# Layer 0's dense MLP on one core: half-width seven-product blocks for three quarters of its first product

## The chip, the cores and the metric

The kernel runs on one core of one Trainium2 chip. Its five engines work in parallel and meet through semaphores: TensorE (PE in the profile; its weight loads are listed apart as PEld), VectorE (DVE), ScalarE (ACT), GpSimd (POOL) and SyncE (SP), which here only issues DMAs. The metric is the device time of one execution in microseconds; the reference point is the median of the timed runs of the kernel before.

## The reference

512 tokens of width 1024 pass two pre-norm residual layers, each a token mixer followed by a dense MLP with a squared ReLU. The part that changes is layer 0's MLP:

```python
def squared_relu_mlp(h, w1, w2):
    a = jax.nn.relu(h @ w1)          # h: 512 x 1024, w1: 1024 x 4096
    return (a * a) @ w2              # w2: 4096 x 1024

    h = rmsnorm(x, norm_ffn_g[i])
    x = x + squared_relu_mlp(h, mlp_w1[i], mlp_w2[i])
```

All data is float32.

## The kernel before

**Three matmuls for one.** A float32 product is made of rounded fp32r parts. Each operand is split into a high part and a remainder, and `mm3` issues three matmuls: high x high, high x low, low x high. Of a weight piece of 128 x 1024 values, ScalarE makes the high part (`nc.scalar.copy(out=p.hi, ...)`, tile wH), and VectorE the remainder (`nc.vector.tensor_sub(out=p.lo, ...)`, tile wL). The matmuls hold a 128x128 block of the weight piece in the array and stream 512 tokens past it: 128x512 is one matmul's output, in one PSUM bank.

**Steps and look-ahead.** The program is a list of `steps`; nearly every step consumes one weight piece (24 matmuls). `run` of a step issues its matmuls, then `advance()` (second halves of earlier evacuations), then `refill()`, and last its own evacuation. `refill` prepares wH up to three and wL up to two pieces ahead:

```python
    def refill():
        n = pos["done"]
        prep(n + (LOOK if n >= 4 else 1), n + (LOOK - 1 if n >= 4 else 1))
```

The order of the calls is the order in each engine's queue, and each engine works its queue in that order. `prep` also loads raw weights, 1 MB each (`load_raws`, `load_part`, on SP's queue), into the pool `bigp` of 14 rotating buffers of 8 KB per partition. The normalised input of a layer lies in `hH` and `hL` (high and remainder, 8 tiles each, in the pool `keep`).

**Layer 0's MLP.** `up(0, q)` makes a quarter (1024 features) of `relu(h @ w1)` in eight steps of 128 features x 512 tokens, each a sum of 8 products over the 1024 inputs; `evac_a` squares it and splits it into `aH` and `aL`. `down(0, q)` multiplies that quarter with w2: eight steps of 128 outputs, each a sum over the quarter's 1024 inputs, so that a step ends in one accumulator. `evac_x(scaled=True)` adds each to the residual `xT`, times the squared norm factor `r2bc` (the factor of the norm is left out of `h` and put back here): two VectorE instructions, `xs` and `xT`. The accumulators are PSUM banks of two pools: `acc` (6) and `mis` (2). In the last `down` each evacuation also makes the next layer's `hH`, `hL` and squares. The order is up 0, up 1, down 0, up 2, down 1, up 3, down 2, down 3. After it the program goes on with `v_unit(0)` of the retention mixer.

Layer 1's MLP already has a Strassen form (`seven`): its VectorE instructions on 128x512 halves (`sa`, `sd`: sums of blocks; `sp`: remainder of such a sum after ScalarE's cast) are of the kinds that the change brings to layer 0.

Of the kernel before, what the change touches and what calls it, by code (L numbers as in the profile page):

```python
# [32 lines left out]
class Raw:  # L33
# [3 lines left out]
    def __init__(self, src, parts=1, adds=(), over=None):  # L37
        self.src, self.parts, self.tile, self.done = src, parts, None, 0
        self.adds, self.over, self.split = adds, over, 0


class Piece:


    def __init__(self, raw, view, shape):
        self.raw, self.view, self.shape = raw, view, shape
        self.hi = self.lo = None
# [33 lines left out]
def trunk(ctx, tc, x, norm_mix_g, norm_ffn_g, a_w_in, a_b_in, a_v_norm_g, a_w_s, a_b_s, a_w_out,  # L81
# [6 lines left out]
    bigp = ctx.enter_context(tc.tile_pool(name="bigp", bufs=14))  # L88
# [4 lines left out]
    ahead = {"raws": 2}  # L93
# [42 lines left out]
    hH = [keep.tile([P, T], F32R, name=f"hH{k}") for k in range(KD)]  # L136
    hL = [keep.tile([P, T], F32R, name=f"hL{k}") for k in range(KD)]
# [18 lines left out]
    def load_part(r):  # L156
        if r.tile is None:
            r.tile = big([P] + list(r.src.shape[1:]), F32, f"raw{raws.index(r)}")
# [5 lines left out]
    def load_raws(upto):  # L164
        while pos["raw"] < min(upto, len(raws)):
            r = raws[pos["raw"]]
            if r.over is not None:
                if r.over.split < 2:
                    return
                r.tile, r.done = r.over.tile, r.parts  # L170
            while r.done < r.parts:
# [10 lines left out]
    def prep(upto, low=None):  # L182

        low = upto if low is None else low
        while pos["piece"] < min(upto, len(order)):
            p = order[pos["piece"]]
            load_raws(raws.index(p.raw) + ahead["raws"])
            prep_tiles(pos["piece"])
            nc.scalar.copy(out=p.hi, in_=p.raw.tile[p.view])  # L189
            pos["piece"] += 1  # L190
        while pos["low"] < min(low, len(order)):
# [4 lines left out]
            load_raws(raws.index(p.raw) + ahead["raws"])  # L196
# [18 lines left out]
    def step(fn, *ps):  # L215
        for p in ps:
            order.append(p)
            if p.raw not in raws:
                raws.append(p.raw)
        steps.append((fn, ps))  # L220
# [15 lines left out]

    def norm_split(k, gcol):

        g = gT[:, gcol + k : gcol + k + 1]
        nc.vector.tensor_scalar_mul(hH[k], xT[k], g)  # L240
        nc.vector.scalar_tensor_tensor(out=hL[k], in0=xT[k], scalar=g, in1=f32(hH[k]), op0=ALU.mult, op1=ALU.subtract)
# [163 lines left out]
    def x_chunk(k, first=None):  # L405
# [3 lines left out]
        if first:  # L409
            g = gT[:, MIX + k : MIX + k + 1]  # L410
# [109 lines left out]
    def out_piece(p, i, h, name, gcol=None, before=None, behind=None):  # L520

        ev = evac_x(gcol)

        def run(p):
            if before:
                before()
            for t in range(2):
                ps = acc(f"{name}{h}_{i}{t}")
                mm_o(p, t, ps, yH[h], yL[h])
# [122 lines left out]
    def up(l, q, behind=None, late=False):  # L652
        pl = pieces_f(mlp_w1[l], (0, D), (1024 * q, 1024 * (q + 1)))
        behind = behind or {}
        i = 0
        if late:
            feat_late(pl[0], pl[1], (evac_a(q, 0), evac_a(q, 1)), f"up{l}{q}")
            i = 2
        while i < 8:
            feat(pl[i], hs, evac_a(q, i), f"up{l}{q}_{i}", behind.get(i))  # L660
            i += 1

    def down(l, q, gcol=None):
        pl = pieces_f(mlp_w2[l], (1024 * q, 1024 * (q + 1)), (0, D))
        ev = evac_x(gcol, True)
        do(flush)
        for i in range(8):
            def evac(ps, i=i):
                ev(i, ps)
                return iter(())  # L670
            feat(pl[i], acts(q), evac, f"dn{l}{q}_{i}")

    nrm_f0 = norm("ffn0", square=True)
    up(0, 0, {2: nxt(nrm_f0), 3: nxt(nrm_f0, 2), 5: nxt(nrm_f0)}, late=True)
    up(0, 1)
    down(0, 0)
    up(0, 2)
    down(0, 1)
    up(0, 3)
    down(0, 2)  # L680
    down(0, 3, gcol=MIX + 8)

# [377 lines left out]
    do(lambda: ahead.update(raws=4))  # L1060
# [15 lines left out]
    for h in range(2):  # L1076
        load_x(0, h)
        load_part(raws[0])
# [4 lines left out]
    load_raws(2)  # L1083
# [68 lines left out]
```

## Time and profile before

| | |
|---|---|
| median of 3 runs | 1392.5 us (1392.06 to 1393.4) |
| the profiled execution | 1392.35 us, span of its instructions 1390.6 us |
| PE busy in the span | 1374.3 us (99%) |
| DVE busy | 845.8 us (61%) |
| ACT busy | 536.2 us (39%) |
| layer 0's MLP in the span | from 291.5 us to 640.7 us |

The span is what the trace covers; the execution's own time is 1.75 us longer. Busy shares are averages over stages; for a change in one stage the rows of that stage count.

### The profile page before, as it was taken

The page shows a single profiled execution, that of the slowest core. Times are in us where ns is not written, and L with a number is a line of the kernel's source. Part 1 is how long each engine was busy: PE and PEld are TensorE (multiplying, and loading weights), DVE is VectorE, ACT ScalarE, POOL GpSimd, SP SyncE. Part 2 cuts the span into 40 slices and gives each one's busy share as a digit, 9 for nine tenths or more (in the row PEclk, how much of TensorE's full clock was granted, in tenths as well). Part 3 has the DMA queues.
Part 4 walks back from the last instruction along what each step waited for, and adds up shares of the span by engine and source line. Part 5 has one row for each costly group of instructions (what it writes and reads, how often), then busy time and mean ns, then how long its engine had stood idle before and what let it go on. Part 6 is the DMA issues. An engine that isn't in the chain of part 4 may idle for free.

```text
span 1390.6 us, 15387 instructions
## 1 busy us (share of the span) xinstructions
PE 1374.3 (99%) x6220; PEld 1142.2 (82%) x6220; DVE 845.8 (61%) x1183; ACT 536.2 (39%) x764; POOL 143.8 (10%) x110
## 2 busy tenths in 40 slices
PE   8999999999999999999999999999999999999996
PEld 7888888888888888888888888888888888888885
DVE  6757756685444444477546574574495665666845
ACT  4646634344413224122333423332333543444522
POOL 3010111130000000012112110100121000100002
PEclk9999999999999999999999999999999999999998
DMA  9051143331323233251012230322434385766511
GB/s 346 3 166 46 47 140 132 121 94 37 113 61 121 91 100 112 76 212 61 31 62 91 77 135 31 120 92 71 141 122 95 105 196 151 174 163 167 133 44 61
DMA packets 114024, 150.99 MB, mean 109 GB/s; under 512 B 2640, under 2 KB 80032, under 8 KB 113696
## 3 DMA queue, kind: packets, MB, share of 16 engines
q1 hardware_dynamic: 107584, 137.41, 29.9%
q0 software_dynamic: 6336, 12.58, 5.4%
q8 instruction: 49, 0.80, 0.2%
q14 instruction: 23, 0.19, 0.0%
q10 hardware_dynamic: 32, 0.01, 0.0%
HBM read 147.89 MB, written 2.10 MB: 108 GB/s over the span
## 4 chain that ended last, share of the span: by engine, by line
PE 95%; DVE 3%; POOL 1%; DMA 0%; ACT 0%; issue 0%; SPq 0%; ACTq 0%; DVEq 0%; POOLq 0%
PE up L228 24%; PE dn L228 13%; PE g L228 6%; PE qk L228 6%; PE vv L228 6%; PE u L228 6%; PE o L228 6%; PE v L228 5%; PE ro L228 5%; PE dt L228 3%; PE av L228 2%; PE sm2a L228 2%; PE sm1a L228 2%; PE sm0a L228 2%; PE sc L228 1%; PE v L573 1%
## 5 line engine op out<-in xcount | busy, mean ns | idle before, releaser
L193 DVE TENSOR_TENSOR wL<-raw,wH 128x1024 fp32r<-128x1024 f32 x257 | 327.4, 1276 | 49.5 <-PE v L228 10.7
L189 ACT CAST wH<-raw 128x1024 fp32r<-128x1024 f32 x257 | 267.4, 1045 | 170.0 <-PE dn L228 101.1
L228 PE MATMUL up<-hH,wH 128*128 128x512 f32 x480 | 187.2, 390 | 0.2 <-ACT xtok L864 0.2
L228 PE MATMUL up<-hL,wH 128*128 128x512 f32 x480 | 186.8, 389 | 0.0
L228 PE MATMUL up<-hH,wL 128*128 128x512 f32 x480 | 186.8, 389 | 0.0
L228 PEld LDWEIGHTS up<-hH,wH 128*128 128x128 f32 x480 | 90.1, 188 | 19.0 <-ACT xtok L864 0.5
L228 PEld LDWEIGHTS up<-hL,wH 128*128 128x128 f32 x480 | 90.1, 188 | 18.8
L228 PEld LDWEIGHTS up<-hH,wL 128*128 128x128 f32 x480 | 90.1, 188 | 18.7
L228 PE MATMUL dn<-aH,wH 128*128 128x512 f32 x256 | 99.6, 389 | 0.0
L228 PE MATMUL dn<-aL,wH 128*128 128x512 f32 x256 | 99.6, 389 | 0.0
L228 PE MATMUL dn<-aH,wL 128*128 128x512 f32 x256 | 99.6, 389 | 0.0
L642 DVE TENSOR_TENSOR aH<-r 128x512 fp32r<-128x512 f32 x40 | 27.7, 692 | 94.5 <-ACT r L640 94.4
L250 POOL TENSOR_TENSOR ssq<-ssq,sq 128x512 f32<-128x512 f32 x28 | 43.5, 1555 | 400.8 <-ACT sq L249 400.5
L512 DVE TENSOR_TENSOR xs<-dn,wide 128x512 f32<-128x512 f32 x32 | 22.1, 691 | 74.6 <-PE dn L228 74.6
L640 ACT ACTIVATE r<-up 128x512 f32<-128x512 f32 x38 | 22.7, 597 | 112.5 <-PE up L228 112.5
L228 PEld LDWEIGHTS dn<-aL,wH 128*128 128x128 f32 x256 | 48.1, 188 | 10.0
L228 PEld LDWEIGHTS dn<-aH,wH 128*128 128x128 f32 x256 | 48.1, 188 | 9.9
L228 PEld LDWEIGHTS dn<-aH,wL 128*128 128x128 f32 x256 | 48.1, 188 | 9.9
L228 PE MATMUL u<-hH,wH 128*128 128x512 f32 x128 | 50.6, 395 | 0.0
L228 PE MATMUL g<-hH,wH 128*128 128x512 f32 x128 | 50.5, 395 | 0.0
L228 PE MATMUL o<-yH,wH 128*128 128x512 f32 x128 | 50.4, 394 | 0.0
L228 PE MATMUL qk<-hH,wH 128*128 128x512 f32 x128 | 50.0, 391 | 0.0
(332 smaller groups left out, 2887.6 us busy)
## 6 DMA issues: line engine op xcount, KB each, us to landing
raw<-in_mlp_w_dram SPq DMA_DIRECT2D x67, 1024.0 KB, 5.2
raw<-in_b_w_in_dram SPq DMA_DIRECT2D x24, 1024.0 KB, 5.0
raw<-in_a_w_in_dram SPq DMA_DIRECT2D x14, 1024.0 KB, 10.9
raw<-in_mlp_w_dram POOLq DMA_DIRECT2D x12, 1024.0 KB, 8.9
raw<-in_a_w_out_dram SPq DMA_DIRECT2D x8, 1024.0 KB, 5.0
raw<-in_b_w_out_dram SPq DMA_DIRECT2D x8, 1024.0 KB, 5.0
raw<-in_a_w_in_dram SPq DMA_DIRECT2D x8, 256.0 KB, 6.7
out_dram<-out SPq DMA_DIRECT2D x8, 256.0 KB, 2.1
```

The source lines that it names most:

```text
L189: nc.scalar.copy(out=p.hi, in_=p.raw.tile[p.view])
L193: nc.vector.tensor_sub(out=p.lo, in0=p.raw.tile[p.view], in1=f32(p.hi))
L228: nc.tensor.matmul(ps, lhsT=a, rhs=b, start=start and i == 0, stop=stop and i == 2, skip_group_check=resumed)
L250: nc.gpsimd.tensor_tensor(out=state["ssq"], in0=state["ssq"], in1=sq, op=ALU.add)
L512: nc.vector.tensor_mul(t, ps, r2bc)
L573: nc.tensor.matmul(accs0[n], lhsT=h[kk][:, n * P : (n + 1) * P], rhs=w, start=kk == 0 and j == 0, stop=kk == 7 and j == 2)
L640: nc.scalar.activation(r, ps, AF.Relu)
L642: nc.vector.tensor_mul(h, r, r)
```

## The change

- The first 1024 of layer 0's 4096 hidden features are computed as before. The other 3072 are six blocks (b = 2 to 7) of 512 features; each is made by `seven_f` of seven products of halves: tokens in two halves of 256 (`HT`), inputs in two halves of 512, features in two halves of 256. A product is 24 matmuls of 128x256. Sums of weight halves (`s1`, `s2`, `s4`, `t3`: tile `sums`, 128x1024) are made by VectorE ahead of the splitting; ScalarE copies three intermediate accumulators out of PSUM (`snap`), and VectorE adds or subtracts them (`quarter`) before the squared ReLU (`evac_a7`).
- `halves` makes the seven input blocks `hb` (high and remainder) once, from a normalised copy `hn` of the residual: it is a generator, advanced by `build` behind chosen steps. Before the first `seven_f` product it has given some of the blocks, and it gives the rest behind the first steps of block 2 and of `dn1`.
- The second product is summed over 512 inputs instead of 1024 (`down_b`, `out_piece`): a step is 24 matmuls still, and ends in two accumulators, both from the pool `mis`. For blocks 0 and 1 (not normalised beforehand) each is added by `xs` and `xT`, for the others by one `xT`.
- The steps of `down_b` of block b - 1 lie between the seven products of block b (`x` is a product, `d1` a step of the second product).
- `hH` and `hL` move from `keep` into `bigp` (now 16 buffers), and raw weights into two buffers of their own (`place`) with one or two more in the MLPs; a raw weight's buffer is reloaded when the last remainder that reads it has been emitted. `load_b` moves to the end of layer 0's MLP.

```diff
-    bigp = ctx.enter_context(tc.tile_pool(name="bigp", bufs=14))
+    bigp = ctx.enter_context(tc.tile_pool(name="bigp", bufs=16))
...
+    def place(r):
+
+        a, shape, name = raws.index(r), [P] + list(r.src.shape[1:]), f"raw{raws.index(r)}"
+        if r.next is not None:
+            return big(shape, F32, name)
+        used = [x.slot for x in raws[:a] if x.slot is not None and not x.free()]
+        if used.count("own") < 2:
+            r.slot = "own"
+            return wts.tile(shape, F32, tag="raw", name=name, bufs=2)
...
+    def lower(low):
         while pos["low"] < min(low, len(order)):
             p = order[pos["low"]]
-            nc.vector.tensor_sub(out=p.lo, in0=p.raw.tile[p.view], in1=f32(p.hi))
-            p.raw.split += 1
+            nc.vector.tensor_sub(out=p.lo, in0=p.src, in1=f32(p.hi))
+            for r in p.raws:
+                r.split += 1
             pos["low"] += 1
-            load_raws(raws.index(p.raw) + ahead["raws"])
+            load_raws()
...
+    def halves(gcol):
...
+        def block(name, c, v, sign=1.0):
+            if c == 0:
+                hb[name] = big([P, 2, 4, HT], F32R, f"hb{gcol}_{name}")
+            hi, lo = [hb[name][:, i, 2 * c : 2 * c + 2, :] for i in range(2)]
+            if sign == 1.0:
+                nc.scalar.copy(out=hi, in_=v)
+                nc.vector.tensor_sub(out=lo, in0=v, in1=f32(hi))
...
+        for c in range(2):
+            nc.vector.tensor_add(out=part(c, 0, 0), in0=part(c, 0, 0), in1=part(c, 1, 1))
+            block("t2", c, part(c, 0, 0))
+            yield
...
+    def seven_f(w, c0, evac, name):
...
+        plan = [("a", piece(0, 0), "n11"), ("c", s1, "t1"), ("a", s2, "t2"), ("b", piece(0, 1), "21"),
+                ("a", total((0, 0), (1, 0), 1), "t3"), ("c", s4, "22"), ("a", piece(1, 1), "t4")]
...
+        def quarter(i, l, bank, key, op):
+            z = zt(f"{name}z{i}{l}")
+            nc.vector.tensor_tensor(out=z, in0=banks[bank], in1=kept[key], op=op)
+            launch(evac(i, l, z, False))
...
+                for u in range(2):
+                    us = slice(u * P, (u + 1) * P)
+                    for k in range(4):
+                        mm3(banks[bank][:, u * HT : (u + 1) * HT], p.hi[:, k, us], p.lo[:, k, us], h[:, 0, k, :], h[:, 1, k, :],
+                            first and u == 0 and k == 0, k == 3, True)
+                advance()
+                refill()
+                then[n]()
...
+    def evac_a7(b):
...
+            r, s = zt(f"ar{b}{i}{l}") if in_psum else v, z2t(f"as{b}{i}{l}")
+            nc.scalar.activation(r, v, AF.Relu)
+            nc.scalar.activation(s, r, AF.Square)
+            nc.vector.tensor_mul(h, half(r), half(r))
+            yield
+            nc.vector.tensor_sub(out=lo, in0=half(s), in1=f32(h))
...
+    dn = down_b(1, scaled=True, behind={0: nxt(h7, 3), 1: nxt(h7, 3), 2: nxt(h7, 2)})
+    for b in range(2, 8):
+        x7 = seven_f(mlp_w1[0], 512 * b, evac_a7(b), f"up0{b}")
+        for m in "d0d1xxd2xxd3xxx" if b == 2 else "xxd0xxd1xxd2xd3":
+            if m == "x":
+                x7.pop(0)()
+                if b == 2 and len(x7) > 4:
+                    do(build)
+            elif m != "d":
+                dn[int(m)]()
+        dn = down_b(b, gcol=MIX + 8 if b == 7 else None)
```

Two places show how the order on the engines changes. The first is TensorE's queue where block 2's first product begins, behind the second accumulator of step dn1_1 (`dn_11`; `hb_n` is the input block n11).

```order
L265 MATMUL dn_11_2856<-aH_4_2514,wH_2742 128x512
L265 MATMUL dn_11_2856<-aL_4_2515,wH_2742 128x512
L265 MATMUL dn_11_2856<-aH_4_2514,wL_2743 128x512
L265 MATMUL up02a<-hb_n_2589,wH_2781 128x256 x2
L265 MATMUL up02a<-hb_n_2589,wL_2782 128x256
```

The matmuls of the first product are now of 256 columns, with as many weight blocks per matmul as before. The second place is VectorE's queue. Before the change, three steps of a second product stand there like this (`xs` and `xT` evacuate an accumulator, `wL` is the remainder of a weight piece two steps ahead):

```order
L512 TENSOR_TENSOR xs_3048<-dn_3_3017,wide 128x512
L513 TENSOR_TENSOR xT_87<-xT_87,xs_3048 128x512
L193 TENSOR_TENSOR wL_3045<-raw_2976,wH_3044 128x1024
L512 TENSOR_TENSOR xs_3080<-dn_4_3051,wide 128x512
L513 TENSOR_TENSOR xT_88<-xT_88,xs_3080 128x512
L193 TENSOR_TENSOR wL_3077<-raw_2976,wH_3076 128x1024
```

After the change, between the two accumulators of step dn1_0 (`dn_00`, `dn_01`), VectorE's queue holds:

```order
L557 TENSOR_TENSOR xs_2804<-dn_00_2791,wide 128x512
L558 TENSOR_TENSOR xT_87<-xT_87,xs_2804 128x512
L776 TENSOR_TENSOR sums<-more_2466 128x1024
L228 TENSOR_TENSOR wL_2782<-raw_2665,wH_2781 128x1024
L746 TENSOR_TENSOR hn_0_2504<-hn_0_2504 128x2x256
L733 TENSOR_TENSOR hb_t_2828<-hn_0_2504,hb_t_2828 128x512
L746 TENSOR_TENSOR hn_1_2505<-hn_1_2505 128x2x256
L733 TENSOR_TENSOR hb_t_2828<-hn_1_2505,hb_t_2828 128x512
L733 TENSOR_TENSOR hb_21_2834<-hn_0_2504,hb_21_2834 128x512
L557 TENSOR_TENSOR xs_2837<-dn_01_2807,wide 128x512
```

A sum of weights and five instructions of `halves` have come between the two `xs`, which free the two `mis` banks. Each `hb_t` remainder follows the sum `hn` that it is made of, with ScalarE's cast between the two.

## Rows read from the trace of the kernel before

**Rows 1.** The page: busy times; then ScalarE groups (busy, mean ns of one | idle).

```profile
PE 1374.3 (99%) x6220; PEld 1142.2 (82%) x6220; DVE 845.8 (61%) x1183; ACT 536.2 (39%) x764; POOL 143.8 (10%) x110
...
L189 ACT CAST wH<-raw 128x1024 fp32r<-128x1024 f32 x257 | 267.4, 1045 | 170.0 <-PE dn L228 101.1
...
L640 ACT ACTIVATE r<-up 128x512 f32<-128x512 f32 x38 | 22.7, 597 | 112.5 <-PE up L228 112.5
```

**Rows 2.** Chain that ended last, in layer 0's MLP: start, us, engine, line, count.

```profile
379.73 43.52 PE dn L228 x192
423.25 43.52 PE up L228 x192
```

**Rows 3.** Windows: layer 0's last norm, then its MLP in two parts.

```profile
core 0: us, PE busy (x) PEld busy (x) DVE busy (x) ACT busy (x) POOL busy (x), PEclk, DMA share, GB/s
264.20:291.50 27.30, 27.30 (x123) 22.62 (x123) 23.08 (x30) 8.46 (x12) 8.64 (x6) 1.00 0.37 116
291.50:379.60 88.10, 88.10 (x390) 72.85 (x389) 49.74 (x69) 36.97 (x53) 5.09 (x4) 1.00 0.23 74
```

**Rows 4.** TensorE's timeline where matmuls of four widths follow each other (start, us).

```profile
717.08 0.33 PE L228 MATMUL av<-pH,vvH 128*128 128x384 f32 x1
717.25 0.34 PE L228 MATMUL av<-pL,vvH 128*128 128x384 f32 x1
...
717.60 0.29 PE L228 MATMUL av<-pH,vvH 128*128 128x256 f32 x1
717.73 0.28 PE L228 MATMUL av<-pL,vvH 128*128 128x256 f32 x1
717.85 0.29 PE L228 MATMUL av<-pH,vvL 128*128 128x256 f32 x1
717.97 0.22 PE L228 MATMUL av<-pH,vvH 128*128 128x128 f32 x1
718.03 0.28 PE L228 MATMUL av<-pL,vvH 128*128 128x128 f32 x1
718.14 0.27 PE L228 MATMUL av<-pH,vvL 128*128 128x128 f32 x1
```

**Rows 5.** VectorE's timeline in layer 1's Strassen part (start, us, idle before).

```profile
1119.45 1.22 DVE L193 TENSOR_TENSOR wL<-raw,wH 128x1024 fp32r<-128x1024 f32 x1
1120.58 0.69 DVE L998 TENSOR_TENSOR sa<-sa,aF 128x512 f32<-128x512 f32 x1
1121.95 0.69 DVE L1012 TENSOR_TENSOR sp<-sa,sp 128x512 fp32r<-128x512 f32 x1 [0.69 <-ACT sp L1011]
1122.56 0.68 DVE L998 TENSOR_TENSOR sa<-sa,aF 128x512 f32<-128x512 f32 x1
```

**Rows 6.** VectorE's timeline in layer 0's second product, and TensorE's beside it.

```profile
472.24 0.69 DVE L512 TENSOR_TENSOR xs<-dn,wide 128x512 f32<-128x512 f32 x1 [2.19 <-PE dn L228]
472.97 0.69 DVE L513 TENSOR_TENSOR xT<-xT,xs 128x512 f32<-128x512 f32 x1
473.58 1.22 DVE L193 TENSOR_TENSOR wL<-raw,wH 128x1024 fp32r<-128x1024 f32 x1
...
472.04 0.39 PE L228 MATMUL dn<-aH,wH 128*128 128x512 f32 x1
```

**Rows 7.** Groups by form, VectorE, 1090 to 1340 us: idle before, releaser.

```profile
L1012 DVE TENSOR_TENSOR sp<-sa,sp 128x512 fp32r<-128x512 f32 x18 | 12.5, 692 | 12.4 <-ACT sp L1011 12.4
```

**Rows 8.** DMA issues: KB each, median us to landing.

```profile
raw<-in_mlp_w_dram SPq DMA_DIRECT2D x67, 1024.0 KB, 5.2
raw<-in_b_w_in_dram SPq DMA_DIRECT2D x24, 1024.0 KB, 5.0
```

**Rows 9.** Window at the end of the span, columns as in rows 3.

```profile
1380.00:1385.00 5.00, 0.00 (x0) 0.00 (x0) 4.79 (x24) 2.12 (x5) 2.52 (x2) 0.76 0.28 105
```

**Rows 10.** TensorE's timeline at the end and at the start of the span.

```profile
1379.54 0.39 PE L228 MATMUL dt<-wH,aL 128*128 128x512 f32 x1
...
7.73 2.06 PE L573 MATMUL v<-wH,hH 128*128 128x512 f32 x4
9.58 1.49 PE L573 MATMUL v<-wL,hH 128*128 128x512 f32 x4
10.91 0.40 PE L573 MATMUL v<-wH,hL 128*128 128x512 f32 x1
```

More of the change, by code (lines that the diff above doesn't have):

```diff
@@ L135, in trunk @@
     xT = [xT2[k // 4][:, k % 4, :] for k in range(KD)]
[L136 to L137 removed]
+    hH, hL = [None] * KD, [None] * KD
     make_identity(nc, ident)
@@ L186, in prep @@
             p = order[pos["piece"]]
-            load_raws(raws.index(p.raw) + ahead["raws"])
+            if p.over is not None:
+                lower(order.index(p.over) + 1)
+            while any(raws.index(r) >= pos["raw"] for r in p.raws):
+                load_raws()
+                if any(raws.index(r) >= pos["raw"] for r in p.raws):
+                    lower(pos["low"] + 1)
             prep_tiles(pos["piece"])
-            nc.scalar.copy(out=p.hi, in_=p.raw.tile[p.view])
+            p.src = p.make() if p.make else p.raws[0].tile[p.view]
+            nc.scalar.copy(out=p.hi, in_=p.src)
             pos["piece"] += 1
+        lower(low)
+    def lower(low):
         while pos["low"] < min(low, len(order)):
             p = order[pos["low"]]
-            nc.vector.tensor_sub(out=p.lo, in0=p.raw.tile[p.view], in1=f32(p.hi))
-            p.raw.split += 1
+            nc.vector.tensor_sub(out=p.lo, in0=p.src, in1=f32(p.hi))
+            for r in p.raws:
+                r.split += 1
             pos["low"] += 1
-            load_raws(raws.index(p.raw) + ahead["raws"])
+            load_raws()
     def launch(g):
@@ new lines, in seven_f, with part, add, make @@
+    def seven_f(w, c0, evac, name):
+        f = [Raw(w[:, c0 + 256 * i : c0 + 256 * (i + 1)].rearrange("(k p) n -> p k n", p=P)) for i in range(2)]
+        def part(i, j):
+            return f[i].tile[:, 4 * j : 4 * j + 4, :]
+        def add(slot, a, b):
+            def make():
+                if "t" not in sums:
+                    sums["t"] = big([P, 2, 4, HT], F32, "sums")
+                t = sums["t"][:, slot]
+                nc.vector.tensor_add(out=t, in0=part(*a), in1=t if b is None else part(*b))
+                return t
+            return make
+        def piece(i, j):
+            return Piece(f[i], (slice(None), slice(4 * j, 4 * j + 4), slice(None)), [P, 4, HT])
+        def total(a, b, slot=0, over=None):
+            return Piece(f[0], None, [P, 4, HT], raws=[f[1]], make=add(slot, a, b), over=over)
+        s1 = total((1, 0), (1, 1))
+        s2 = total((0, 0), None, over=s1)
+        s4 = total((0, 1), None, over=s2)
+        plan = [("a", piece(0, 0), "n11"), ("c", s1, "t1"), ("a", s2, "t2"), ("b", piece(0, 1), "21"),
+                ("a", total((0, 0), (1, 0), 1), "t3"), ("c", s4, "22"), ("a", piece(1, 1), "t4")]
+        banks, kept = {}, {}
+        def snap(key, bank, scale=1.0):
+            kept[key] = z2t(f"{name}{key}")
+            nc.scalar.activation(kept[key], banks[bank], AF.Copy, scale=scale)
+        def quarter(i, l, bank, key, op):
+            z = zt(f"{name}z{i}{l}")
+            nc.vector.tensor_tensor(out=z, in0=banks[bank], in1=kept[key], op=op)
+            launch(evac(i, l, z, False))
+        then = [lambda: snap("s", "a", -1.0), lambda: snap("e", "c"), lambda: snap("v", "a"),
+                lambda: quarter(0, 0, "b", "s", ALU.add), lambda: quarter(1, 1, "a", "e", ALU.subtract),
+                lambda: quarter(0, 1, "c", "v", ALU.subtract), lambda: launch(evac(1, 0, banks["a"], True))]
+        def one(n):
+            bank, _, hname = plan[n]
+            def run(p):
+                first = bank not in banks
+                if first:
+                    banks[bank] = acc(f"{name}{bank}")
+                h = hb[hname]
+                for u in range(2):
+                    us = slice(u * P, (u + 1) * P)
[5 more added lines that the diff above has]
+                then[n]()
+            return run
+        return [lambda n=n: step(one(n), plan[n][1]) for n in range(7)]
@@ new lines, in down_b @@
+    def down_b(b, gcol=None, scaled=False, behind=None):
+        pl = pieces_o(mlp_w2[0], (512 * b, 512 * (b + 1)), (0, D))
+        behind = behind or {}
+        return [lambda i=i: out_piece(pl[i], i, b, "dn", gcol, act=(aH, aL), bank=mis, scaled=scaled, behind=behind.get(i)) for i in range(4)]
+    nrm_f0 = norm("ffn0", square=True)
+    h7 = halves(FFN)
+    build = nxt(h7)
+    pl = pieces_f(mlp_w1[0], (0, D), (0, 1024))
+    feat_late(pl[0], pl[1], (evac_a(0, 0), evac_a(0, 1)), "up00")
@@ new lines, in trunk @@
+    do(nxt(nrm_f0))
+    for i in (2, 3):
+        feat(pl[i], hs, evac_a(0, i), f"up00_{i}", nxt(nrm_f0))
+    do(flush)
+    do(lambda: extra.append(big([P, 2048], F32, "more0")))
+    dn = down_b(0, scaled=True, behind={1: build, 2: build})
+    for i in range(4):
+        feat(pl[4 + i], hs, evac_a(0, 4 + i), f"up00_{4 + i}", (lambda: (next(nrm_f0, None), nxt(h7, 4)())) if i == 0 else build if i < 3 else None)
+        dn[i]()
+    do(flush)
+    do(lambda: extra.append(big([P, 2048], F32, "more1")))
@@ L684, in trunk @@
+    for d in dn:
+        d()
     bw = b_w_in[0]
```

138 lines of the change are left out of this document (87 added, 51 removed).

## The prediction

> **What bounds the kernel now.** I read the page first. TensorE is busy for 1374 of 1390.6 us, VectorE for 61% and ScalarE for 39% [rows 1]. The chain that ended last then shows where layer 0's MLP stands: 192 matmuls of its second product take 43.52 us and 192 of its first 43.52 us, 0.2267 us each, with nothing between them [rows 2]; the windows agree, TensorE being busy for 88.10 of 88.10 us [rows 3]. So in this stage fewer TensorE columns shorten the kernel, as long as VectorE and ScalarE deliver in time. VectorE has half of such a window left (49.74 of 88.10 us) [rows 3], but that is an average; I therefore follow its queue where the change packs most into it.
>
> **What TensorE saves.** The first product of six blocks took 6 x 96 = 576 matmuls of 512 columns: 576 x 0.2267 = 130.6 us. It becomes 6 x 7 x 24 = 1008 matmuls of 256. The trace has such matmuls in `av`: their starts lie 0.13, 0.12 and 0.12 us apart, those of 384 columns 0.17, those of 128 columns 0.06 and then 0.11 [rows 4]. Halving the columns does not halve the time: 0.2267 and 0.17 lie on a line that reaches 0.12 at 256 columns, so some 0.013 us per matmul is not columns. Bounds are 0.11 (the step of 128 columns, which columns alone do not explain; weight loads come no closer there) and 0.13; I take 0.121, nearest to the two steps in the middle of the run and to the line. 1008 x 0.121 = 122.0 us: **TensorE saves 8.6 us**, an eighth of the arithmetic less the fixed part of 432 more matmuls. The second product has 768 matmuls of 512 columns as before.
>
> **What it costs on VectorE.** Per block of the later kind (b = 3 to 7) VectorE has 11 remainders wL and 4 sums of 128x1024, and 19 instructions of 512 (3 quarters, 4 aH, 4 aL, 8 xT). Back to back, the next instruction starts 1.13 us after a 128x1024 one and 0.61 after a 128x512 one [rows 5]. That is 15 x 1.13 + 19 x 0.61 = 28.5 us, and 3 waits for ScalarE of 0.76 (below), 31 us in all, beside 7 x 2.90 + 4 x 5.44 = 42.1 us of TensorE: hidden, with two steps of look-ahead. If that cover were gone it would be the new bound of 187 us of the stage.
>
> The place without cover is the start of the blocks, where `halves` still gives its blocks, `dn1` still needs two evacuation instructions per accumulator, and the sums of weights begin. I follow VectorE's queue from the end of the first accumulator of step dn1_0 to the remainder that the third matmul of dn2_0 loads. In between TensorE has 0.5 + 3 steps of the second product, 9 seven-product steps and two matmuls: 3.5 x 5.44 + 9 x 2.90 + 0.45 = 45.6 us. VectorE has 61 instructions:
> - 18 of 128x1024 (12 wL, 6 sums): 18 x 1.13 = 20.3 us;
> - 43 of 128x512 (8 xs, 8 xT, 16 of `halves`, 3 quarters, 4 aH, 4 aL): 43 x 0.61 = 26.2 us;
> - 8 times xT behind the xs that it reads, 0.73 instead of 0.61 us [rows 6]: 1.0 us;
> - 9 times a result goes to ScalarE and comes back with nothing between in the queue: six sums of `hn` (sum, cast, remainder) and three quarters (quarter, ReLU, aH). Layer 1 has that pattern: from `sa` to `sp` 1.37 us instead of 0.61 [rows 5], 0.69 us idle in each of 18 [rows 7]: 9 x 0.76 = 6.8 us;
> - the remainders of block 22 wait for a cast that stands behind the cast of a weight sum and a copy on ScalarE (1.05 and 0.60 us each [rows 1]), while VectorE has one wL: 1.4 us, an estimate;
> - 0.2 us from TensorE's next matmul to xs [rows 6], and as much back, an estimate: 0.4 us.
>
> That is 56.1 us against 45.6: **TensorE waits 10.5 us** between dn1_1 and dn2_0. The waits should come in this order. The second half of dn1_1 needs a bank of `mis`, of which there are two; `xs` of dn1_0's second accumulator frees it and now stands behind a sum, a wL and five instructions of `halves`: 0.2 + 0.73 + 0.61 + 1.13 + 1.13 + 2 x 1.37 + 3 x 0.61 + 0.69 = 9.1 us after the bank before it, where TensorE has 5.44: 3.6 us. Behind `xs` in that queue stand the wL of the next steps, so dn1_2 waits for its wL by some 2.4, dn1_3 by some 2.5, and block 3's first two products and dn2_0 share the other 2. The chain is unbroken: each accumulator that VectorE evacuates in it ended before its turn.
>
> Here a rule of the Trainium skill speaks against the change. The row shows that an instruction of 0.69 us lets the next one start after 0.61, before it has ended [rows 5]. The page "VectorE: DVE Perf Modes" (Terms, DRAIN) says that a flush follows every operation and the next cannot issue until the pipe is empty. By that the 61 instructions would cost their full 1.22 and 0.69 us, some 5 us more, and the kernel would end near 1399; the row decides.
>
> **The other edits.** The start of `halves` (eight instructions that make `hn`, and the blocks n11 and t1) lies beside dn0, where the two products alternate in whole steps of 5.44 us; the latest free bank there comes 1.4 us early by the same counting, so it costs nothing; bounds 0 and 3 us. The last block's four steps each end in two norms: the mixer's last output step has the same form, and TensorE was busy for all of its window (27.30 us [rows 3]): nothing. ScalarE has 18 more casts of 1.05 us, some 20 of 0.6 net, spread over 300 us: nothing, it is at 39%. Raw weights have two buffers outside the MLPs, and a reload waits for the last remainder that reads its buffer; by the order, the first cast of the new weight is due two steps (10.9 us) later, and a megabyte lands in 5.0 to 5.2 us [rows 8]; SP's queue holds nothing else but the two tables of `load_b`, whose buffers are free by then. Hidden, with about 5 us to spare; a late weight would cost at most its 5 us. I take nothing, and keep 0 to 5 for the range.
>
> **The sum** against the profiled execution of 1392.35 us (0.15 under the median of 1392.5): 1392.35 - 8.6 + 10.5 = 1394.25, say **1394.3 us**. The change gives TensorE less to do and takes about as much back in waits.
>
> **The rivals.**
> - *The waits stay short: faster.* If the nine round trips through ScalarE cost VectorE nothing, the chain is 49.3 us and the wait 3.7: 1392.35 - 8.6 + 3.7 = 1387.5. Against it: all 18 such places in layer 1 show the idle time [rows 7]. For it: two of my terms are estimates, and the queue has 45 us to catch up. It is faster by over 0.2% once the waits are under 5.9 us.
> - *Half-wide matmuls cost more.* At 0.13 us, the largest step [rows 4], the first product takes 131.0 us and saves nothing; TensorE's share of the chain is then 1.9 us longer and the wait 8.6: 1401.3. At 0.125 it is 1397. For it: weight loads are as many as matmuls and come at least 0.11 apart in rows 4.
> - *The clock falls in the wait.* The granted clock averages 0.76 in a window of 5 us that begins after the last matmul (started at 1379.54) [rows 9, 10]: full at first, then half. A wait of 3.6 us could do the same. At the start, after idle time, eight matmuls take from 7.73 to 10.91, 3.18 us [rows 10], instead of 8 x 0.2267 = 1.81: a fall costs about 1.4 us. But VectorE's chain goes on meanwhile, and the next wait shrinks by as much: 1394.3 to 1396, 1398 if it falls in each of three waits. The Trainium skill ("TensorE: Matmul & The Clock Gate", "Why this matters for your kernels") warns of just such gaps between bursts of matmuls; no row before shows a gap of this length inside the kernel.
> - *Raw weights come late* in the retention layer or layer 1's MLP: 5 us for one, 1399.
>
> **How the numbers follow.** Chances: the forecast 0.52, short waits 0.20, dearer matmuls 0.12, the clock 0.10, late weights 0.06. The forecast's own range is 1392.5 to 1396.5 (waits of 9 to 12.5 us). For 8 in 10 the range runs from 1388.5, leaving out the shorter half of the short waits, to 1399.5, leaving out matmuls near 0.13. A measurement of this kernel tells a change from none at about 0.2%, 2.8 us. Faster is the short waits, 0.20; the forecast lies for three quarters within 0.2% (up to 1395.3), and with a part of the clock's and the matmuls' cases that makes 0.46 the same; slower 0.34.
>
> **What would show it.** Right: the starts of up02's matmuls 0.12 us apart; TensorE idle before dn1_1's second accumulator, released by VectorE's `xs`, and before dn1_2, dn1_3 and block 3, released by wL, some 10 us in all; VectorE without idle time there but for 0.7 us waits on ScalarE's casts; from dn2_1 to the retention layer no wait. Wrong: under 6 us of waits there, steps of 0.13, or idle time of TensorE in any other stage.

## The result and the profile after

The changed kernel takes **1395.27 us** (median of 11 runs, 1393.73 to 1396.21) and the kernel before 1391.97 us (11 runs, 1390.64 to 1393.4): a ratio of 1.0024, 95% interval 1.0014 to 1.0033. It is slower by 3.3 us, or 0.24%, where the bound was 0.2%: the interval holds both sides of it. Its profiled execution took 1395.05 us, with a span of 1393.3 us.

The page's busy line of after, which answers to [rows 1]:

```profile
PE 1371.1 (98%) x6652; PEld 1157.9 (83%) x6652; DVE 931.0 (67%) x1289; ACT 572.0 (41%) x814; POOL 142.8 (10%) x110
```

TensorE has 432 more matmuls than before and is busy for 3.2 us less, and yet the span is 2.7 us longer: what was saved came back as idle time and, as shown below, as slow matmuls, and somewhat more. The windows of after, by stage (span of the stretch, then each engine's busy time and count, the granted clock, DMA share, GB/s), answer to [rows 3]:

```profile
291.10:360.40 69.30, 69.30 (x306) 57.26 (x305) 55.86 (x82) 27.50 (x39) 4.98 (x4) 1.00 0.35 109
360.40:416.93 56.53, 50.63 (x302) 44.83 (x300) 48.47 (x62) 24.30 (x34) 0.00 (x0) 0.91 0.26 91
416.93:617.60 200.67, 200.61 (x1256) 182.11 (x1257) 142.42 (x164) 85.81 (x109) 0.00 (x0) 1.00 0.32 105
617.60:643.40 25.80, 25.41 (x113) 20.67 (x112) 21.81 (x28) 7.82 (x12) 7.97 (x6) 1.00 0.39 143
643.40:1045.50 402.10, 401.10 (x1846) 334.85 (x1845) 247.69 (x375) 137.68 (x200) 54.28 (x40) 1.00 0.24 79
```

From the start of the MLP (291.1 us) to 360.4 us TensorE is never idle, and none of the stages behind the MLP is longer than before (the retention layer: 402.1 us in both). Nearly all of the loss lies in the second window, from dn1 to the start of block 3; the last block has 0.4 us of idle time. The waits of TensorE from 285 to 650 us (us in total, times, longest):

```profile
PE dn L265 <- DVE xs L557: 3.5, 1, 3.5
PE dn L265 <- DVE wL L228: 2.2, 2, 1.8
PE dn L265 <- DVE xT L560: 0.4, 1, 0.4
PE up03c L265 <- DVE wL L228: 0.3, 1, 0.3
```

That is 6.4 us of idle time. What is lost is twice that: TensorE's saving (9.6 us, below) and the 3.0 us by which the MLP is longer. The windows around the longest wait and behind the next show the rest in their seventh number, the granted clock:

```profile
365.40:369.30 3.90, 0.40 (x2) 0.00 (x0) 3.18 (x6) 2.60 (x4) 0.00 (x0) 0.89 0.01 2
369.30:375.30 6.00, 6.00 (x16) 4.89 (x17) 5.28 (x8) 0.62 (x2) 0.00 (x0) 0.50 0.00 0
394.30:399.20 4.90, 4.84 (x14) 3.84 (x15) 4.17 (x6) 3.53 (x6) 0.00 (x0) 0.65 0.76 236
```

TensorE counts as busy there, but at the lower of its two levels, 1.2 GHz instead of 2.4, for all of six microseconds and for most of another five. Before, the granted clock was full throughout the MLP. The timeline of TensorE at the first wait (start, length, instruction, idle time ahead of it and its releaser):

```profile
365.18 0.39 PE L265 MATMUL dn<-aL,wH 128*128 128x512 f32 x1
365.41 0.39 PE L265 MATMUL dn<-aH,wL 128*128 128x512 f32 x1
369.30 0.80 PE L265 MATMUL dn<-aH,wH 128*128 128x512 f32 x1 [3.51 <-DVE xs L557]
369.89 0.63 PE L265 MATMUL dn<-aL,wH 128*128 128x512 f32 x1
370.32 0.63 PE L265 MATMUL dn<-aH,wL 128*128 128x512 f32 x1
```

The step from 365.41 to 369.30 is 3.89 us where 0.227 is usual, a wait of 3.67 us; behind it the steps are 0.59 and 0.43. And this is what VectorE does meanwhile (its timeline, the first instruction of the stretch, the piece in front of `xs`, and the last one, which dn2_0's third matmul waits for):

```profile
360.40 0.69 DVE L557 TENSOR_TENSOR xs<-dn,wide 128x512 f32<-128x512 f32 x1 [0.96 <-PE dn L265]
...
365.99 0.68 DVE L746 TENSOR_TENSOR hn<-hn 128x512 f32<-128x512 f32 x1
367.35 0.69 DVE L733 TENSOR_TENSOR hb_t<-hn,hb_t 128x512 fp32r<-128x512 f32 x1 [0.69 <-ACT hb_t L732]
367.96 0.69 DVE L733 TENSOR_TENSOR hb<-hn,hb 128x512 fp32r<-128x512 f32 x1
368.56 0.69 DVE L557 TENSOR_TENSOR xs<-dn,wide 128x512 f32<-128x512 f32 x1
...
415.71 1.22 DVE L228 TENSOR_TENSOR wL<-raw,wH 128x1024 fp32r<-128x1024 f32 x1
```

The `xs` that frees the bank runs at 368.56, behind the instructions of `halves`. From 360.40 to the end of the last wL at 416.93 the queue takes 56.5 us. Measured on TensorE, from its first matmul behind dn1_0's first accumulator (360.20) to dn2_0's third (416.99), the stretch takes 56.8 us.

### The profile page after: what moved, and what is told of

Its sections match the earlier page's. It is cut to its first block, busy times and chain, and to the rows that moved or that the text cites. A ratio compares the mean times of both kernels' runs of the same rounds, so it can differ in the third digit from the quotient of the medians.

```text
span 1393.3 us, 16442 instructions
## 1 busy us (share of the span) xinstructions
PE 1371.1 (98%) x6652; PEld 1157.9 (83%) x6652; DVE 931.0 (67%) x1289; ACT 572.0 (41%) x814; POOL 142.8 (10%) x110
## 4 chain that ended last, share of the span: by engine, by line
PE 93%; DVE 5%; POOL 1%; issue 1%; ACT 1%; DMA 0%; SPq 0%; DVEq 0%; ACTq 0%; POOLq 0%
PE up L265 14%; PE dn L265 12%; PE g L265 6%; PE qk L265 6%; PE vv L265 6%; PE u L265 6%; PE o L265 6%; PE v L265 5%; PE ro L265 5%; PE dt L265 3%; PE av L265 2%; PE sm2a L265 2%; PE sm1a L265 2%; PE sm0a L265 2%; PE sc L265 1%; PE v L619 1%
## 5 line engine op out<-in xcount | busy, mean ns | idle before, releaser
L228 DVE TENSOR_TENSOR wL<-raw,wH 128x1024 fp32r<-128x1024 f32 x206 | 259.4, 1262 | 47.3 <-issue 13.5
L221 ACT CAST wH<-raw 128x1024 fp32r<-128x1024 f32 x206 | 214.6, 1045 | 79.0 <-PE dt L265 12.0
L265 PE MATMUL up<-hH,wH 128*128 128x512 f32 x288 | 112.5, 391 | 0.2 <-ACT xtok L1059 0.2
L265 PE MATMUL up<-hL,wH 128*128 128x512 f32 x288 | 112.1, 389 | 0.0
L265 PE MATMUL up<-hH,wL 128*128 128x512 f32 x288 | 112.1, 389 | 0.0
L265 PEld LDWEIGHTS up<-hH,wH 128*128 128x128 f32 x288 | 54.1, 188 | 11.5 <-ACT xtok L1059 0.5
L265 PEld LDWEIGHTS up<-hH,wL 128*128 128x128 f32 x288 | 54.1, 188 | 11.4
L265 PEld LDWEIGHTS up<-hL,wH 128*128 128x128 f32 x288 | 54.0, 188 | 11.2
L228 DVE TENSOR_TENSOR wL<-more,wH 128x1024 fp32r<-128x1024 f32 x45 | 56.9, 1267 | 0.0
L221 ACT CAST wH<-more 128x1024 fp32r<-128x1024 f32 x45 | 46.9, 1043 | 18.3 <-PE dn L265 8.7
```

The lines of the kernel that those rows point to most:

```text
L221: nc.scalar.copy(out=p.hi, in_=p.src)
L228: nc.vector.tensor_sub(out=p.lo, in0=p.src, in1=f32(p.hi))
L265: nc.tensor.matmul(ps, lhsT=a, rhs=b, start=start and i == 0, stop=stop and i == 2, skip_group_check=resumed)
```

## The experiments

My theory, the **chain**: from dn1_0 to dn2_0 VectorE's queue, its idle time included, sets the end of the stretch, whatever wait TensorE shows and at whatever clock it runs in between. The rival, the **local** view: each wait has its own cause and price (a bank freed late, a late wL, a fall of the clock), and each can be taken away by itself. In all kernels but one (8) the span from the first matmul of `vv` to the end is 750.0 us within 0.1, so that the length of the MLP (first matmul of `up00a` to first of `vv`, in the timeline of the profiled run, one execution of each kernel) shows each effect more finely than the total.

| kernel | median us | ratio to before, 95% interval | MLP, us |
|---|---|---|---|
| before | 1392.0 | | 349.2 |
| after | 1395.27 | 1.0024 (1.0014 to 1.0033) | 352.3 |
| 1 xs first | 1399.18 | 1.0054 (1.0041 to 1.0067) | 355.5 |
| 2 filled wait | 1395.12 | 1.0022 (1.0013 to 1.0031) | 352.0 |
| 3 halves on GpSimd | 1394.95 | 1.0020 (1.0012 to 1.0029) | 352.0 |
| 4 no seven products | 1397.62 | 1.0040 (1.0027 to 1.0054) | 353.5 |
| 5 remainders a turn later | 1394.54 | 1.0018 (1.0010 to 1.0027) | 351.0 |
| 6 and earlier | 1389.36 | 0.9982 (0.9973 to 0.9991) | 346.3 |
| 7 and late aH, banks of acc | 1385.70 | 0.9956 (0.9943 to 0.9968) | 343.1 |
| 8 no seven products, banks of acc | 1397.05 | 1.0032 (1.0019 to 1.0045) | 349.2 |
| 9 as 7, sums first | 1383.57 | 0.9940 (0.9928 to 0.9953) | 340.9 |
| 10 six more in the chain | 1399.85 | 1.0058 (1.0046 to 1.0071) | 357.0 |
| 11 eight more later | 1394.98 | 1.0023 (1.0013 to 1.0033) | 352.1 |
| 12 no seven products, long last sums | 1391.98 | 1.0000 (0.9991 to 1.0009) | 349.2 |

**1. The bank freed first.**

```diff
                 mm_o(p, t, ps, hi[h], lo[h])
+                if first:
+                    ev(2 * i + t, ps)
                 if t == 1:
                     advance()
...
+                if not first:
+                    ev(2 * i + t, ps)
```

> The four steps of dn1 evacuate their second accumulator (xs, xT) ahead of the remainders, sums and instructions of halves that the step issues, not behind them; VectorE has the same instructions in another order. Chain theory: what counts is VectorE's whole queue from 360.4 us (56.5 us up to the wL of dn2_0's third matmul) against 45.4 us of TensorE, so the 3.7 us in front of dn1_1's second accumulator goes away and comes back in front of dn1_2, dn1_3 and block 3: time as after, 1395.3 (1394 to 1396.5). Rival, a local wait: the bank is the cause, and with it the 3.7 us and the fall of the granted clock behind it (some 3 us) go for good: 1388.5 (1387 to 1391).

It is 3.9 us slower than after, which neither view gave. The wait for the bank is gone and 3.7 us (from start to start) stand in front of a wL of up02c instead: later in the queue, as the chain has it, though not at the steps that I had named. TensorE's line for it:

```profile
PE up02c L265 <- DVE wL L228: 3.9, 2, 3.6
```

But VectorE also got more idle time, since `xs` now comes up in its queue before its accumulator has ended. VectorE's waits from 352 to 425 us, first of this kernel:

```profile
DVE xs L557 <- PE dn L265: 5.6, 5, 1.5
DVE hb_t L736 <- ACT hb_t L735: 4.1, 6, 0.7
```

and of after:

```profile
DVE xs L557 <- PE dn L265: 2.4, 2, 1.4
```

The queue from the first `xs` to the wL of dn2_0 takes 59.8 us in place of 56.5: 3.2 us more idle, 3.2 us more of MLP. I had left out of the theory that the order of a queue changes its idle time.

**2. The wait filled, so that the clock stays full.**

```diff
-            mm3(ps, p.hi[:, k, ts], p.lo[:, k, ts], bH[:, k, :], bL[:, k, :], k == 0, k == 3)
+            mm3(ps, p.hi[:, k, ts], p.lo[:, k, ts], bH[:, k, :], bL[:, k, :], k == 0, k == 3 and not fill)
+        for f in range(fill):
+            nc.tensor.matmul(ps, lhsT=zero, rhs=bH[:, 0, :], start=False, stop=f == fill - 1)
```

> Fifteen more matmuls of 512 columns, of a tile of zeros, are added to dn1_1's first accumulator, so that TensorE is busy for 3.4 of the 3.7 us in which it waits for the bank of the second; nothing else changes. The granted clock should then stay full from 365 us to at least the wait in front of dn1_3. Chain theory: VectorE's queue sets when the later wL come, so the slow matmuls were free and the later waits grow by what TensorE now gains: 1395.3 (1394.3 to 1396.3), with some 3 us more of waiting for wL in front of dn1_2, dn1_3, block 3 and dn2_0. Rival: the fall of the clock is a cost on the path, 3.0 to 4.8 us: 1390.5 to 1392.3.

The chain, to 0.15 us. The windows of this kernel over the same stretches as above show the clock full:

```profile
365.40:369.30 3.90, 3.90 (x18) 3.00 (x16) 2.99 (x5) 2.54 (x5) 0.00 (x0) 1.00 0.04 12
369.30:375.30 6.00, 5.89 (x37) 5.21 (x37) 5.24 (x9) 0.88 (x2) 0.00 (x0) 1.00 0.00 0
```

and its waits the price in another place, more than twice the idle time for wL:

```profile
PE dn L268 <- DVE wL L231: 4.5, 3, 2.2
PE up03c L268 <- DVE wL L231: 0.8, 1, 0.8
PE up03a L268 <- DVE wL L231: 0.7, 1, 0.7
```

The half clock of after cost nothing: TensorE was slow where it would have waited. Run 11 below shows the same unasked: in the same three windows its clock was 1.00, 0.72 and 1.00, where after had 0.89, 0.50 and 0.65, and its MLP is as long (352.1 us). The Trainium skill ("TensorE: Matmul & The Clock Gate", "Why this matters for your kernels") advises against idle gaps between bursts of matmuls, since the clock falls behind them. It did fall here, but the advice has a price only where TensorE sets the end.

**3. Sums and remainders of halves on GpSimd.**

```diff
-                nc.vector.tensor_sub(out=lo, in0=v, in1=f32(hi))
+                nc.gpsimd.tensor_tensor(out=lo, in0=v, in1=f32(hi), op=ALU.subtract)
```

The same for the eight sums of `hn`.

> The sums of hn and the remainders of t1, t2, 21, t3, 22 and t4 in halves (8 sums, 12 remainders of 512) go from VectorE to GpSimd, where a tensor_tensor of that size takes 1.29 to 1.52 us in this trace and which is idle from 311 to 600 us. VectorE's chain loses 16 x 0.61 and six round trips of 0.76: 56.5 - 14.3 = 42.2 us against TensorE's 45.4. Chain theory: the waits and both falls of the clock go, 11 us: 1384.3 (1383 to 1386). Rival, the two engines hinder each other or GpSimd hands the blocks on late: VectorE's instructions beside GpSimd's last longer than 0.69 and 1.22 us, or TensorE waits for hb from GpSimd; then 1388 to 1396.

The rival: no gain. VectorE lost 16 instructions and its busy time from 360.4 to 396.5 us fell only from 30.61 to 29.23 us. The timeline, GpSimd (POOL) and VectorE:

```profile
370.07 1.08 DVE L558 TENSOR_TENSOR xT<-xT,xs 128x512 f32<-128x512 f32 x1
370.54 3.99 POOL L733 TENSOR_TENSOR hb<-hn,hb 128x512 fp32r<-128x512 f32 x2
371.06 2.31 DVE L776 TENSOR_TENSOR sums<-raw,sums 128x1024 f32<-128x1024 f32 x1
373.30 2.31 DVE L228 TENSOR_TENSOR wL<-raw,wH 128x1024 fp32r<-128x1024 f32 x1
374.49 2.27 POOL L753 TENSOR_TENSOR hn<-hn 128x512 f32<-128x512 f32 x1
...
381.65 1.45 DVE L228 TENSOR_TENSOR wL<-sums,wH 128x1024 fp32r<-128x1024 f32 x1 [6.04 <-ACT wH L221]
```

Beside GpSimd a 128x1024 instruction takes up to 2.31 us instead of 1.22, and `xT` 1.08 instead of 0.69. Only `xs`, with one input from PSUM, keeps its 0.68 (six of them average 680 ns). The Trainium skill says this ("GPSIMD Engine Reference", "Specifications": SBUF interfaces are shared with VectorE where an instruction has two SBUF inputs; "SBUF — State Buffer", "SBUF: two separate sides": whichever begins first keeps the port for its whole instruction), and the rows agree. The 6.04 us in the last row are a second loss: ScalarE's cast of that weight sum stood behind a cast of `hb_t` that waited for GpSimd.

**5, 6, 7 and 9. Idle time out of the queue, and work ahead of the stretch.** The remainder of a block is issued one turn after its cast (5); five instructions go ahead of dn1 (6); aH goes one turn behind its ReLU and the last block takes six banks (7); the next block's sum goes ahead of the remainder, and one turn moves from dn1_0 to dn1_1 (9). The main pieces, as run 9 has them, against after:

```diff
             if sign == 1.0:
                 nc.scalar.copy(out=hi, in_=v)
-                nc.vector.tensor_sub(out=lo, in0=v, in1=f32(hi))
...
+            late.append((hi, lo, v, sign))
+
+        def remainder():
+            for hi, lo, v, sign in late:
...
         for c in range(2):
             nc.vector.tensor_sub(out=part(c, 0, 0), in0=part(c, 0, 0), in1=part(c, 0, 1))
+            remainder()
             block("t1", c, part(c, 0, 0))
             yield
...
             nc.scalar.activation(s, r, AF.Square)
+            yield
             nc.vector.tensor_mul(h, half(r), half(r))
...
-    return [lambda i=i: out_piece(pl[i], i, b, "dn", gcol, act=(aH, aL), bank=mis, scaled=scaled, behind=behind.get(i)) for i in range(4)]
+    return [lambda i=i: out_piece(pl[i], i, b, "dn", gcol, act=(aH, aL), bank=acc if b == 7 else mis, scaled=scaled, behind=behind.get(i)) for i in range(4)]
...
-    dn = down_b(0, scaled=True, behind={1: build, 2: build})
+    dn = down_b(0, scaled=True, behind={1: build, 2: build, 3: build})
...
-    dn = down_b(1, scaled=True, behind={0: nxt(h7, 3), 1: nxt(h7, 3), 2: nxt(h7, 2)})
+    dn = down_b(1, scaled=True, behind={0: build, 1: nxt(h7, 2), 2: nxt(h7, 2)})
```

Ahead of dn0_3, up00_7 takes two turns of `halves` as well.

> Each remainder of halves is issued one turn after its cast, behind the next block's sum and other work, so VectorE no longer stands idle for the six casts (4.1 us) and the cast of block 22 (1.0 us); the same instructions otherwise. Chain theory (VectorE's queue with its idle time sets the end of the stretch, whatever the order of TensorE's waits): 5.1 us less, 1390.2 (1389.3 to 1391.3). Rival, the round trips are covered by other waits, or the later remainders hold up something else: 1393.5 to 1396.

Only 0.7 us faster: my edit was bad, not the theory. Two turns are issued at once in several places, so that a remainder still came right behind its own cast, and five idle times of 0.69 us (3.4 in all, from 4.1) stayed. What did leave the queue, 0.7 us of these and the 1.0 us of block 22's cast, less 0.3 of a new wait in front of an `xs`, is about the 1.2 us by which the MLP is shorter than after's.

> As the run without round trips, and five more instructions of halves (block t2 and the last remainder of t1) go ahead of 360 us, behind up00_7 and dn0_3, where VectorE of the kernel after stands idle for 6.3 of 20 us, as well as the last remainder behind a later product. Chain theory: another 5 x 0.61 to 6 x 0.61 us, some 3.4 us: 1386.8 (1385.8 to 1388.5), no wait for a bank of mis before dn1_1. Rival: dn0_3's bank comes later and the wait moves ahead of dn1_0: 1389 to 1391.

5.9 us faster than after and the first to beat the kernel before, but 2.6 us short of the forecast, outside its range and inside the rival's. The rival's wait ahead of dn1_0 is not there; a wait of 1.0 us for the bank of dn1_1, which I had excluded, is. Of the idle times that run 5 kept, one of 0.69 us is left in this stretch. VectorE's waits, 355 to 425 us, show what took its place:

```profile
DVE xs L557 <- PE dn L265: 1.3, 1, 1.3
DVE hb_t L742 <- ACT hb_t L734: 0.7, 1, 0.7
```

An `xs` now waits 1.3 us for its accumulator, as in run 1, and the first `xs` of dn1_0 starts 0.5 us later, counted from the start of the MLP, than in after, since VectorE is busier ahead of it. With the 0.7 us that is 2.5 us.

> As the early run, and two more edits: the aH of a quarter is issued one turn after its ReLU (three idle times of 0.70 us in block 2), and the last block's four steps take their banks from the six of acc, where none of the first product stands any more (0.55 + 0.11 us in front of dn7). Chain theory: what is left of the waits, some 3 us, less 2.1, and less 0.66: 1384.0 (1383.2 to 1386), that is TensorE's saving of 9.6 us with next to nothing given back. Rival: aH a turn later makes dn2_0 wait for aL, or ScalarE becomes late: 1386 to 1389.

3.7 us more, and inside its range. The two edits were priced at 2.8 us; the MLP is 3.2 us shorter than in run 6.

> As the best run so far (1385.7), with the next block's sum ahead of the remainder of the block before, so that this remainder no longer follows its own cast directly, and one of the two turns behind dn1_0 moved to dn1_1. That run still has two idle times of 0.69 us for casts in VectorE's queue, and 2.7 us of TensorE's waits in this stretch (1.3 for the bank of dn1_1, 0.8 and 0.4 for the wL of dn1_3 and dn2_0, 0.2 elsewhere). Chain theory: 1.4 to 2.0 us less, 1384.0 (1383.3 to 1384.6). Rival, these waits have another source: 1385.5 to 1386.5.

**1383.57 us**, within its range, 8.5 us under the kernel before and 11.7 under after. Its profile lists no wait of TensorE in the MLP, and the window of its stretch (the first `xs` of dn1_0 to just before dn2_0's third matmul) is full at full clock:

```profile
360.80:406.60 45.80, 45.72 (x302) 41.61 (x300) 44.41 (x57) 22.52 (x31) 0.00 (x0) 1.00 0.32 111
```

45.8 us where after had 56.5, with VectorE at 97%: the two engines are matched here.

**10 and 11. The same kind of work added in two places.**

```diff
-                nc.vector.tensor_sub(out=lo, in0=v, in1=f32(hi))
+                for _ in range(4 if name == "21" else 1):
+                    nc.vector.tensor_sub(out=lo, in0=v, in1=f32(hi))
...
-            nc.vector.tensor_sub(out=lo, in0=half(s), in1=f32(h))
+            for _ in range(3 if b == 4 else 1):
+                nc.vector.tensor_sub(out=lo, in0=half(s), in1=f32(h))
```

The first piece alone is run 10, the second run 11.

> The kernel after, with the two remainders of block 21 done four times each in place of once (the same values): six instructions of 512 more in VectorE's queue between dn1_0 and dn1_2, nothing else. Chain theory: 6 x 0.61 = 3.7 us later, all of it: 1398.9 (1398.0 to 1400), with the start of dn2_0 3.7 us later in the profile. Rival, only the waits that TensorE shows count, and what its slow matmuls cover is free: 0 to 2 us, 1395.3 to 1397.3.

> The kernel after, with the four remainders aL of block 4 done three times each (the same values): eight instructions of 512 more, 4.9 us of VectorE, spread over the steps of one later block. Chain theory and the prediction's step on the later blocks (31 of 42.1 us, so 11 us of slack): nothing, 1395.3 (1394.5 to 1396), no wait of TensorE between 425 and 600 us. Rival, the slack is no slack because work comes in lumps: up to 4.9 us, 1397 to 1400.

Six instructions in the chain cost 4.6 us, 4.8 in the MLP; eight in a later block cost nothing. That tells the two views apart best. Run 10 is 0.9 over its forecast since a repeated remainder starts 0.73 us after the one before, not 0.61 (four of them, the last of 0.69 us, take 2.87 us): 6 x 0.73 = 4.4, and 0.5 us more of idle time for `xs`. In its timeline:

```profile
367.96 2.87 DVE L734 TENSOR_TENSOR hb<-hn,hb 128x512 fp32r<-128x512 f32 x4
```

Where run 11 works, VectorE has 125.67 busy us of 170 and TensorE all of them:

```profile
430.00:600.00 170.00, 170.00 (x1066) 154.40 (x1065) 125.67 (x147) 70.44 (x89) 0.00 (x0) 1.00 0.32 105
```

**4, 8 and 12. The change without the seven products.** The edit of run 4; 8 also takes the last block's banks from `acc`, and 12 sums the last two blocks over 1024.

```diff
-        x7 = seven_f(mlp_w1[0], 512 * b, evac_a7(b), f"up0{b}")
-        for m in "d0d1xxd2xxd3xxx" if b == 2 else "xxd0xxd1xxd2xd3":
...
+        pq = pieces_f(mlp_w1[0], (0, D), (512 * b, 512 * (b + 1)))
+        for i in range(4):
+            feat(pq[i], hs, evac_a(b // 2, 4 * (b % 2) + i), f"up0{b}_{i}")
+            dn[i]()
```

> Without the seven products: blocks 2 to 7 of the first product are made as in before, 24 matmuls of 512 columns per 128 rows and no halves, while the rest of the change stays: second product in sums of 512 through two banks, in turns with the first, buffers, order, loads. Forecast of my own sum: these other edits cost nothing, and this is the kernel before, 1392.0, less 0.4 us at the start, plus 0.5 to 0.7 in front of the last step of the MLP: 1391.5 to 1393. Rival: the turns, the two banks or the larger number of evacuations cost by themselves 2 us or more: 1394 or more, and then the seven products gain where I have them lose.

1397.62, and so "the other edits cost nothing" looked wrong. But its only waits are two in front of the last steps of the MLP, for `xs` (3.6 us). There this kernel differs from after: its last block is scaled, with two evacuations per accumulator and the norms behind them. The profiled run was the fastest of its five; what the others, 1.6 to 3.3 us slower, had more is not in a trace.

> Without the seven products, once more, and with the last block's banks from acc: in the run without the seven products two waits of 1.9 and 2.5 us stood in front of the last two steps of the MLP alone, for xs, since there the last block still had two evacuation instructions and its norms behind two banks. If these are all that it cost: 1391.0 to 1392.5, as before (1392.0), and the other edits cost nothing. Rival: the turns or the loads cost elsewhere: 1394 or more.

Missed: with more banks the MLP is as short as before, and the waits come behind it (for the wL of `vv`, 2.6 us in two), and the granted clock averages 0.88 there:

```profile
291.50:640.70 349.20, 349.20 (x1542) 289.11 (x1540) 214.93 (x282) 108.58 (x139) 11.41 (x8) 1.00 0.32 107
640.70:655.00 14.30, 11.74 (x44) 8.90 (x43) 13.99 (x16) 5.35 (x7) 5.90 (x4) 0.88 0.01 1
```

VectorE is busy for 13.99 of 14.30 us: the lag of its queue moved past the bank to the next thing that waits for it, as in the chain theory. With the last two blocks summed as in before that lag does not arise:

> Without the seven products, a third time: blocks 2 to 7 of the first product as before, the second product of blocks 0 to 5 in sums of 512 through two banks, in turns with the first, and of blocks 6 and 7 at the end in one sum of 1024, as before. That leaves out what delayed both earlier runs of this kind: in their last block VectorE had two evacuations and the two norms for each accumulator, 6 us and more per step of 5.44 (its 128x1024 instructions took 2.3 us there, beside GpSimd's sums of squares). If nothing else of these edits costs: 1391 to 1392.5, as before (1392.0), and the seven products with what they need are all of the 3.3 us. Rival: turns, banks, buffers or loads cost by themselves: 1394 or more.

1391.98 against 1391.99: turns, buffers, loads and, up to block 5, sums of 512 through two banks cost nothing by themselves. What the change gains and loses lies in the seven products and in what they ask of VectorE, but for the last block, whose two banks this run leaves out: its 0.7 us in after are accounted for below.

## Why the prediction was right

**Matmuls of 256 columns.** Three of them take 0.36 us in TensorE's timeline of after:

```profile
391.04 0.28 PE L265 MATMUL up02b<-hb,wL 128*128 128x256 f32 x1
391.16 0.40 PE L265 MATMUL up02b<-hb,wH 128*128 128x256 f32 x2
391.40 0.28 PE L265 MATMUL up02b<-hb,wL 128*128 128x256 f32 x1
```

The step is 0.120, not 0.121, so TensorE saves 130.6 - 1008 x 0.120 = 9.6 us, 1.0 more than predicted; the rival of dearer matmuls is out.

**VectorE's chain.** Predicted 56.1 us, with 0.4 for the two hand-overs between the engines; between the same points the trace has 56.8 (the 56.5 above is VectorE's part alone). Its idle times were as costed: six casts 4.1 us, three quarters 2.1, block 22's cast 1.0 against an estimate of 1.4. The rival of short waits is out with it. Run 10 shows that it is this chain that sets the end. By the rule that the Trainium skill states ("VectorE: DVE Perf Modes", Terms, DRAIN) it would have been some 5 us longer; the rows, with 0.61 us from start to start, do not bear it out.

**TensorE's wait.** Predicted 10.5; 56.8 less the 45.4 that TensorE needs at the measured step is 11.4. The place and size of the first wait were right (3.6 forecast, 3.67 measured, for `xs`). The next ones were not: dn1_2 showed none, dn1_3 2.0 instead of 2.5, and 0.9 in all in front of up03c and dn2_0. The difference is the half clock: from start to start the 11.4 us are 6.7 of waits and 4.7 of slower steps. So the sign "some 10 us" of idle time was not met: the list has 6.0 in this stretch, close to the "under 6 us" that was to show the prediction wrong, and only run 2, where the clock is full and the time the same, shows that the waits were there in another form. The half clock was a rival, at 0.10, that came true in its mechanism, twice. I took 1.4 us of slower TensorE for a fall, and the first one took 2.8; I put its price in the kernel's time at 0 to 1.7 us, more with a third fall, and run 2 measures it as nothing.

**The last block.** I took nothing, by the mixer's last output step; that was wrong by 0.66 us (0.55 and 0.11 in two steps), and idle time in another stage was one of my signs of being wrong. The step of the argument that failed is the likeness: that output step has six banks and this one two. VectorE's timeline, then GpSimd's and TensorE's:

```profile
634.63 0.75 DVE L285 SCALAR_TENSOR_TENSOR hL<-xT,gT,hH 128x512 fp32r<-128x512 f32 x1
...
636.86 1.83 DVE L285 SCALAR_TENSOR_TENSOR hL<-xT,gT,hH 128x512 fp32r<-128x512 f32 x1
638.62 1.21 DVE L228 TENSOR_TENSOR wL<-more,wH 128x1024 fp32r<-128x1024 f32 x1
639.75 0.68 DVE L560 TENSOR_TENSOR xT<-xT,dn 128x512 f32<-128x512 f32 x1
```

```profile
636.85 1.29 POOL L294 TENSOR_TENSOR ssq<-ssq,sq 128x512 f32<-128x512 f32 x1 [0.31 <-ACT sq L293]
...
640.48 0.50 PE L265 MATMUL dn<-aH,wH 128*128 128x512 f32 x1 [0.39 <-DVE xT L560]
```

The norm's hL takes 1.83 us instead of 0.75, beside GpSimd's sum of squares (`ssq`), and the `xT` that frees the bank stands behind it. With six banks (runs 7 and 9) the wait is gone.

**The rest.** The start of `halves` cost nothing (69.30 of 69.30 us busy), nor did the later blocks (200.61 of 200.67; run 11) nor the raw weights (402.1 us of retention layer in both).

**The sum** for the MLP: -9.6 + 11.4 + 0.7 = +2.5, measured +3.0. The rest, some 0.6 us, lies in steps that are up to a tenth longer each, spread from 300 us to the end of the MLP; I did not resolve why. The forecast was -8.6 + 10.5 = +1.9. Its two large terms were 1.0 and 0.9 us off in opposite directions: that they cancel is luck. What is left of the error, 1 us, is the last block and those small steps. Faster than before was within reach with the same arithmetic (run 9), by an order of VectorE's queue that I had not looked for.

## What to carry to other kernels

Where the saved engine waits for another, count the other's whole queue over the stretch, idle time for round trips included: here that queue was forecast within 0.7 us, while the waits that TensorE showed, one by one, gave neither the cause nor what removing one would bring (runs 1 and 2). Idle time leaves such a queue when a result is used one turn later and when work moves ahead to where the engine has room; with six banks for the last block (0.7 us) that was worth 11.7 us here, more than the 9.6 us that the new arithmetic saves TensorE. Handing the work to another engine is to be tried only after a look at what the two do to each other's instructions.

## What the runs showed of the hardware

The granted clock fell to half in a wait of 3.7 us and again just behind one of 2.0 us (0.50 over 6.0 us and 0.65 over 4.9 us); in run 2 waits of 2.2 and 2.3 us passed without a fall, and in run 1 one of 2.8 us (1.00 from 395.2 to 405.0 us). The length of a wait alone does not tell here whether the clock falls. VectorE and GpSimd nearly stood in each other's way by whole instructions: 2.31 us instead of 1.22, and 2.27 instead of 1.29 on GpSimd. An instruction that overwrites the output of the one just before it started 0.73 us after it instead of 0.61 (run 10).
